# A fourth buffer for gathered U vectors, a later place for the last block's decoding, and no forced U work between the last G groups

## The chip, the cores and the metric

The kernel runs on one core of one Trainium2 chip. The metric is the device time of one execution in microseconds (us); three executions of the kernel before are at hand, and their median stands for it. Beside them there is one profiled execution, with a page and a trace: busy times, waits and the timeline of each engine. The engines are TensorE (PE, matmuls; PEld, its weight loads), VectorE (DVE), ScalarE (ACT), GpSimd (POOL, here an issuer of gathers) and SyncE (SP, which issues most transfers). Each works through its own list of instructions in the order in which the program emits them, and waits on semaphores for the others.

## The reference: what is computed

The program is one transformer-like layer on 512 tokens of width 1024 in float32: a layer norm, a mixer of 16 state-space heads and 8 latent-attention heads, a second norm, and a channel mixer with a residual and a last norm. The change touches the channel mixer, PEER, alone. It has 16384 experts; every token picks 16 of them in each of 8 heads.

```
q = (xb @ w_query)...; s = scores against 2 x 128 sub-keys
sv, si = lax.top_k(s, K)                          # 16 of 128, for both halves
top_s, top_pos = lax.top_k(cand_s, K)             # 16 of 256 candidate pairs
expert_idx = jnp.take_along_axis(cand_i, top_pos, axis=-1)
gate = jax.nn.softmax(top_s, axis=-1)
u = jnp.take(u_table, expert_idx, axis=0)
act = gelu(jnp.einsum('td,thkd->thk', xb, u))
v = jnp.take(v_table, expert_idx, axis=0)
return jnp.einsum('thk,thkd->td', gate * act, v)
```

So for token t the output is the sum over its 128 chosen experts e of gate * gelu(u_e . x_t) * v_e.

## The kernel before, in words

**Two ways to the same sum.** For the first three blocks of 128 tokens (384 tokens, NT) the kernel computes all experts densely: act = gelu(U x) for 128 chunks of 128 experts, times a matrix G of gates (zero where an expert wasn't chosen), times V. A float32 product is made of three matmuls of a high and a low part (mm3, L72 to L75). For the last block, and for the last 32 tokens (UG) of block 2 in the U step, the kernel gathers the rows of the tables that are needed and multiplies them on DVE. So a U matmul has 352 columns (NU), and V matmuls have 512 columns for three blocks and two halves.

**U chunk** (u_half, u_chunk, L1292 to L1305): 24 matmuls into one of two PSUM banks (pu), then a Gelu on ACT (L1301) that writes the act tile and frees the bank. **V chunk** (v_chunk, L1536): 18 matmuls into six banks that hold the sum over all 128 chunks. It needs P = act * G (DVE, L1493, and a small copy on ACT, L1495), the high part Ph (ACT, L1513) and the low part Pl (DVE, L1521). Weights for both come through one stream (Stream, L81): SP loads a tile of 128 x 1024 into one of three raw buffers (L92), ACT makes the high part (L110), DVE the low one (L120), two items ahead of PE.

**G, in 48 groups** (build_g, L1186): for each 8 tokens DVE makes one-hot matrices (L1194) and multiplies them with the gates (L1201); PE makes 16 small matmuls (L1220, L1221) into two PSUM tiles; ACT evicts them into a staging tile stg (L1223). For even groups from 2 to 42 (LOWA) DVE makes half of the product only, and ACT the other half with eight copies (L1226), issued behind the eviction of the group before. Every fourth group the staging tile is stored from ACT's queue, a small part to gs0 (L1229, 128 KB) and the rest to gsp (L1230, 1920 KB). V's stage reads them back, gt, four chunks at a time (load_g, L1401 to L1405; the first two loads read gs0).

**Gathered U vectors** (ug_index, ug_fetch, ug_dots, L1114 to L1144): 32 indirect transfers by POOL (L1130) into the tile urow with three buffers, and for each a product with a sum on DVE (L1136). The fetch that uses a buffer again is issued behind the product that frees it. One product is drawn per group, two in the groups 4, 8, 12, 16 and 20, and two earlier in the decoding. When all are done, their pool is closed and its room becomes a second pool for act tiles.

**Who orders the work.** The order of instructions is fixed when the program is built. drive (L1346) keeps two accounts in microseconds, tm[0] for PE and tm[1] for DVE: a U half chunk adds T_U/2 to the first, and its split 1.2 to the second; a group adds 0.95 to the first and 1.9 or 2.42 to the second, a gathered product 1.2. A half chunk is emitted as long as PE's account isn't ahead of DVE's, or, in build_g, as long as none has been emitted since the last group (least = 1). U chunks may go up to KEEP while one pool of act tiles exists and up to LEAD - RES = 54 with two.

**From G to V.** Behind the last group come, in the order of the program (L1465 to L1546): the loads for the decoding of block 3 (late3, L1101, decode, L1032: from L1105 and L1107), the first two gt loads, the decoding itself, dealt out by pump between U chunks 54 and 55, then P, Ph and Pl for V chunks 0 and 1, then pairs of a U chunk (from 56) and a V chunk (from 0). pump (L1241) draws so many microseconds (by the program's own figures) of the generator gather behind each chunk. When the decoding is done, gather goes on to 256 fetched rows for block 3 (L1431, five buffers), one DVE product each (L1442 for U, L1448 for V), spread over what remains of the U and V chunks (L1566 to L1571). The decoding uses Exp (L1060), the U chunks Gelu, and ACT loads a table between the two.

Of the kernel before, what the change touches and what calls it, by code (L numbers as in the profile page):

```python
# [11 lines left out]
F32 = mybir.dt.float32  # L12
# [19 lines left out]
UG = 32  # L32
NU = NT - UG
LEAD = 56
KEEP = 45
RES = 2
LASTC = 120
T_U = 3.87
T_Q = 6.3
ROWS = 5  # L40
ENDU = 12
# [13 lines left out]
def tile_block(ctx: ExitStack, tc: tile.TileContext, I, out):  # L55
# [1070 lines left out]

    def ug_fetch(n):
        if n < UG:
            UR[n] = ug.tile([128, D], F32, name="urow", bufs=3)
            G.indirect_dma_start(out=UR[n], out_offset=None, in_=I["u"],  # L1130
                                 in_offset=bass.IndirectOffsetOnAxis(ap=UR["ix"][:, n:n + 1], axis=0))

    def ug_dots():
        for n in range(UG):
            r = UR.pop(n)
            V.scalar_tensor_tensor(r, r, 1.0, UR["x"], op0=OP.mult, op1=OP.mult, accum_out=UR["hd"][:, n:n + 1])  # L1136
# [49 lines left out]
    def build_g():  # L1186
        jij = gb.tile([128, 4, 4, 128, 2], F16, name="ij")

        def hot(n):
            ijT, gT, gL = GT[n // 16]  # L1190
            r = n % 2
            col = ijT[:, n % 16 // 2, r].rearrange("p e (q c) -> p (e q) c", c=2)
            b2 = [128, 8, 128, 2]
            V.tensor_tensor(jij[:, 2 * r:2 * r + 2].rearrange("p e q i c -> p (e q) i c"), iotaE[:, None].to_broadcast(b2),  # L1194
                            col[:, :, None, :].to_broadcast(b2), op=OP.is_equal)
            oj, oi = jij[:, 1 + r], jij[:, 3 * r]
            g = gb.tile([128, 2, 4, 128, 2], F16, name="g", bufs=2)
# [3 lines left out]
            V.tensor_tensor(g[:, :ne], oi[:, None].to_broadcast(b4), gv[:, :, :, None, :].to_broadcast(b4), op=OP.mult)  # L1201
            low = [(g[:, 1, t // 2, :, t % 2], oi[:, t // 2, :, t % 2], gL[:, n % 16, t:t + 1]) for t in range(8)]
            return oj, g[:, 0], g[:, 1], low if ne == 1 else []

        nxt = hot(0)
        dots, head = UR["dots"], ug_head()
        tm[1] += 3.0
        yield 2.6
        for n in range(48):
            b, g = divmod(n, 16)  # L1210
            oj, oi, g1, _ = nxt
            if n < 47:
                nxt = hot(n + 1)
            if g % 4 == 0:
                stg = gs[n // 4 % 2].tile([128, 128, 32], F32, name="stg")
            for hf in range(2):
                ps = pw()
                for t in range(4):
                    q, c = hf * 2 + t // 2, t % 2
                    T.matmul(ps[:, t * 128:(t + 1) * 128], oj[:, q, :, c], oi[:, q, :, c], start=True, stop=False)  # L1220
                    T.matmul(ps[:, t * 128:(t + 1) * 128], oj[:, q, :, c], g1[:, q, :, c], start=False, stop=True)  # L1221
                q0 = g % 4 * 8 + hf * 4
                A.activation(stg[:, :, q0:q0 + 4],  # L1223
                             ps.rearrange("p (t i) -> p i t", t=4), AF.Copy, scale=1.0 / GSC)
            for o, i, z in nxt[3] if n < 47 else ():
                A.activation(o, i, AF.Copy, scale=z)  # L1226
# [105 lines left out]
    load_sk(0)  # L1332
    load_sk(1)
    tm = [0.0, 0.0]

    def step_u():
        e = len(UO)
# [55 lines left out]
    gb = pool("gb", side="right")  # L1393
    UR["w"] = gb.tile([UG, 128], F32, name="uw")
    UR["m"] = gb.tile([UG, 2], F32, name="um")
    drive(build_g(), 1)
    close(gb, *gs)
    vst = pool("vst")
    gt = {}
# [4 lines left out]
            src, q0 = (gs0, q * 4) if q < 2 else (gsp, q * 4 - 8)  # L1404
            nc.sync.dma_start(gt[q], src[:, :, q0:q0 + 4, :].rearrange("b j i t -> j b i t"))  # L1405

    GS = [-1, 0, 0]

    def gather():
        yield from late3()  # L1410
        ijg = IJG.pop(3)
        ix = gp_.tile([128, 128], I32, name="ix")
        f = lambda z: z.rearrange("p h k -> p (h k)")
        V.scalar_tensor_tensor(ix, f(ijg[:, 0]), 128.0, f(ijg[:, 1]), op0=OP.mult, op1=OP.add)
        g3 = gp_.tile([128, 128], F32, name="g3")
        V.tensor_copy(g3, f(ijg[:, 2]))
        close(*late, ijp)
        yield 0.5
        gp2 = pool("gp2", side="right")
        x3 = gp2.tile([128, D], F32, name="x3")  # L1420
        nc.sync.dma_start(x3, xsp[3])
        hd = gp2.tile([128, 128], F32, name="hd")
        ac = gp2.tile([128, D], F32, name="ac")
        V.memset(ac, 0.0)
        R = {}
        yield 0.1

        def fetch(s):
            if s < 256:
                R[s] = gp2.tile([128, D], F32, name="row", bufs=ROWS)  # L1430
                G.indirect_dma_start(out=R[s], out_offset=None, in_=I["u"] if s < 128 else I["v"],  # L1431
                                     in_offset=bass.IndirectOffsetOnAxis(ap=ix[:, s % 128:s % 128 + 1], axis=0))
# [103 lines left out]
    def v_chunk(c):  # L1536
# [4 lines left out]
        for b in range(3):  # L1541
            v_mm(b, c, hl)

    vc = 0
    for c in range(2):
        v_hi(c, v_prep(c))  # L1546
# [4 lines left out]
    while vc <= LASTC:  # L1551
# [171 lines left out]
```

## Time and profile before

| | |
|---|---|
| three executions | 1608.65, 1609.93, 1613.17 us |
| median | 1609.93 us |
| the profiled execution's own time | 1608.0 us |
| its span, first to last instruction | 1605.9 us |
| mean granted TensorE clock | 0.995 |
| U vectors gathered (first fetch to last product) | 561.4 to 707 us |
| groups of G on PE | 583.5 to 774 us |
| first V matmul | 798.8 us |
| PE busy in 700 to 750, 750 to 800, 800 to 850 us | 49.71, 35.05, 50.00 us |

How to read it: times in the trace count from the first instruction, so a point in the trace and the span compare directly, and the execution's own time is 2.1 us more. A row of the timeline has the start, the duration, the engine (SPq, ACTq and POOLq are the issuing sides of these engines), the line, the operation, and output and inputs by name. Brackets say how long the engine stood idle ahead of it and which instruction or transfer ended that. A row of a view by windows has, for each stretch, the busy time (and count) of PE, PEld, DVE, ACT and POOL, then the granted clock, the busy share of the transfer engines and GB/s. A row of waits has the waiting line, the line waited for, the total, the number and the longest. Matmul rows overlap: what counts for PE's pace is the distance of two starts.

### The profile page before, as it was taken

How to read it: one execution, taken by the hardware profiler on the slowest of the kernel's cores; microseconds unless marked ns; L12 is line 12 of the kernel's file. 1: busy time of each engine (PE TensorE's matmuls, PEld its weight loads, DVE VectorE, ACT ScalarE, POOL GpSimd, SP SyncE). 2: the span in 40 equal slices, each digit the busy share in tenths (PEclk: the TensorE clock that was granted, in tenths of full speed). 3: DMA queues.
4: the chain of work that ended last, by engine and by line, in shares of the span. 5: the costliest groups of instructions: out<-in, count | busy, mean ns of one | idle time of the engine just before them, and what ended most of it. 6: DMA issues, size and time to landing. Idle time of an engine off the chain costs nothing.

```text
span 1605.9 us, 24098 instructions
## 1 busy us (share of the span) xinstructions
PE 1572.7 (98%) x8699; PEld 1381.7 (86%) x8699; DVE 1344.6 (84%) x2545; ACT 754.8 (47%) x1409; POOL 547.7 (34%) x400
## 2 busy tenths in 40 slices
PE   9999999999999999999699999999999999999997
PEld 7887888887888999989599999999999999888886
DVE  8978677647799998989678888888888888988887
ACT  5564467731333457779433343333333433433342
POOL 0000032500245134410045555555555455544310
PEclk9999999999999999999899999999999999999999
DMA  6342132473433479887599999999999999999974
GB/s 248 97 155 91 47 78 64 138 249 118 134 93 91 142 244 343 330 307 255 202 333 344 362 346 349 340 354 355 338 338 365 343 337 356 372 327 351 327 254 143
DMA packets 154556, 403.88 MB, mean 251 GB/s; under 512 B 13037, under 2 KB 65965, under 8 KB 152645
## 3 DMA queue, kind: packets, MB, share of 16 engines
q1 hardware_dynamic: 104948, 213.19, 39.7%
q0 software_dynamic: 45888, 163.73, 27.9%
q10 hardware_dynamic: 3600, 25.43, 4.0%
q8 instruction: 68, 1.11, 0.3%
q14 instruction: 52, 0.42, 0.1%
HBM read 368.40 MB, written 31.80 MB: 249 GB/s over the span
## 4 chain that ended last, share of the span: by engine, by line
PE 77%; DVE 11%; issue 5%; ACT 2%; POOL 2%; DMA 2%; DVEq 0%; SPq 0%; ACTq 0%; POOLq 0%
PE va L1530 11%; PE va L1531 11%; PE va L1534 11%; PE pu L73 8%; PE pu L75 8%; PE pu L74 8%; PE pa L74 3%; PE pa L75 3%; PE pa L73 3%; POOL urow L1130 2%; PE pw L74 1%; PE pw L75 1%; PE pw L73 1%; DVE t L1003 1%; DVE ti L1007 1%
## 5 line engine op out<-in xcount | busy, mean ns | idle before, releaser
L110 ACT ACTIVATE wih<-wir 128x1024 fp32r<-128x1024 f32 (+2 forms) x269 | 277.7, 1033 | 279.2 <-DMA wir<-v 113.5
L120 DVE TENSOR_TENSOR wil<-wir,wih 128x1024 fp32r<-128x1024 f32 (+1 forms) x235 | 284.1, 1210 | 97.9 <-ACT wih L110 40.0
L75 PE MATMUL pu<-XTH,wil 128*128 128x352 f32 x1008 | 325.2, 323 | 0.5 <-DVE wil L120 0.5
L73 PE MATMUL pu<-XTH,wih 128*128 128x352 f32 x896 | 292.8, 327 | 5.8 <-ACT act L1301 5.8
L74 PE MATMUL pu<-XTL,wih 128*128 128x352 f32 x896 | 289.3, 323 | 0.0
L1531 PE MATMUL va<-wil,Ph 128*128 128x512 f32 x726 | 283.6, 391 | 0.0
L1431 POOL DMA_INDIRECT row<-u,ix x128 | 191.6, 1497 | 215.5 <-DVE row L1442 138.6
L1431 POOL DMA_INDIRECT row<-v,ix x128 | 183.5, 1434 | 191.6 <-DVE ac L1448 170.2
L75 PEld LDWEIGHTS pu<-XTH,wil 128*128 128x128 f32 x1008 | 190.0, 188 | 0.9 <-DVE wil L120 0.9
L73 PEld LDWEIGHTS pu<-XTH,wih 128*128 128x128 f32 x896 | 168.8, 188 | 10.1 <-ACT act L1301 6.4
L1530 PE MATMUL va<-wih,Ph 128*128 128x512 f32 x438 | 171.5, 392 | 4.5 <-ACT Ph L1513 4.5
L74 PEld LDWEIGHTS pu<-XTL,wih 128*128 128x128 f32 x896 | 169.0, 189 | 2.8
L1448 DVE SCALAR_TENSOR_TENSOR ac<-row,hd,ac 128x1024 f32<-128x1024 f32 x128 | 164.0, 1281 | 2.7 <-DMA row<-v,ix 0.6
L1531 PEld LDWEIGHTS va<-wil,Ph 128*128 128x128 f32 x726 | 136.7, 188 | 26.0
L1442 DVE SCALAR_TENSOR_TENSOR row<-row,x 128x1024 f32<-128x1024 f32 x128 | 150.1, 1221 | 2.8 <-DMA row<-u,ix 2.8
L1301 ACT ACTIVATE act<-pu 128x352 f32<-128x352 f32 x126 | 58.2, 462 | 167.3 <-PE pu L75 162.9
L1534 PE MATMUL va<-wih,Pl 128*128 128x512 f32 x438 | 135.3, 390 | 0.0
L110 ACT ACTIVATE wihx<-wir 128x1024 fp32r<-128x1024 f32 x67 | 71.0, 1059 | 121.0 <-DMA wir<-v 84.8
L120 POOL TENSOR_TENSOR wil<-wir,wih 128x1024 fp32r<-128x1024 f32 (+3 forms) x34 | 70.5, 2081 | 154.5 <-PE pw L75 100.2
L1530 PE MATMUL va<-wihx,Ph 128*128 128x512 f32 x288 | 112.3, 390 | 0.0
L120 DVE TENSOR_TENSOR wil<-wir,wihx 128x1024 fp32r<-128x1024 f32 x62 | 75.8, 1223 | 41.0 <-issue 27.9
L1530 PEld LDWEIGHTS va<-wih,Ph 128*128 128x128 f32 x438 | 82.5, 188 | 20.7 <-ACT Ph L1513 4.8
(500 smaller groups left out, 3230.6 us busy)
## 6 DMA issues: line engine op xcount, KB each, us to landing
wir<-ut SPq DMA_DIRECT2D x128, 512.0 KB
wir<-v SPq DMA_DIRECT2D x128, 512.0 KB
gsp<-stg ACTq DMA_DIRECT2D x12, 1920.0 KB
gt<-gsp SPq DMA_DIRECT2D x30, 768.0 KB
wir<-wo SPq DMA_DIRECT2D x26, 512.0 KB
wir<-wf SPq DMA_DIRECT2D x18, 512.0 KB
wir<-wqr SPq DMA_DIRECT2D x16, 512.0 KB
de<-acd POOLq DMA_DIRECT2D x8, 512.0 KB
```

Of the source, the lines that this page charges most:

```text
L73: T.matmul(ps, lh, rh, start=start, stop=False)
L74: T.matmul(ps, lh, rl, start=False, stop=False)
L75: T.matmul(ps, ll, rh, start=False, stop=stop)
L110: A.activation(h, r, AF.Copy)
L120: self.lo(n).tensor_tensor(l, r, h, op=OP.subtract)
L1301: A.activation(ACT[c], ps, AF.Gelu)
L1431: G.indirect_dma_start(out=R[s], out_offset=None, in_=I["u"] if s < 128 else I["v"], in_offset=bass.IndirectOffsetOnAxis(ap=ix[:, s % 128: ...
L1442: V.scalar_tensor_tensor(r, r, 1.0, x3, op0=OP.mult, op1=OP.mult, accum_out=hd[:, s:s + 1])
L1448: V.scalar_tensor_tensor(ac, r, hd[:, s - 128:s - 127], ac, op0=OP.mult, op1=OP.add)
L1530: T.matmul(va[b][e], Ph[b], h[:, cs], start=c == 0, stop=False)
L1531: T.matmul(va[b][e], Ph[b], l[:, cs], start=False, stop=False)
L1534: T.matmul(va[b][e], Pl[b], h[:, cs], start=False, stop=c == 127)
```

## The change

One more buffer for gathered U vectors (UROWS = 4), so the first act pool has 42 tiles in place of 45 and the second 14 in place of 11; the two-product groups become 2, 5, 8, 11, 14 and 17; T_U is 3.9 in place of 3.87. From group 32 on no half chunk is forced between groups (least becomes 0). The generator of block 3's decoding and gathering starts behind V's chunk 0 and not ahead of U chunk 54: the gt loads come first on SP, U chunks 54 and 55 follow with nothing between them, and the first pump is the one in V's loop, at 2.1 us for a chunk and 4.2 for a pair. The definitions of load_g to v_chunk move up unchanged, and are left out below.

```diff
-KEEP = 45
+KEEP = 42
+UROWS = 4
-T_U = 3.87
+T_U = 3.9
...
-        for n in range(3):
+        for n in range(UROWS):
             ug_fetch(n)
...
-            UR[n] = ug.tile([128, D], F32, name="urow", bufs=3)
+            UR[n] = ug.tile([128, D], F32, name="urow", bufs=UROWS)
...
-            ug_fetch(n + 3)
+            ug_fetch(n + UROWS)
...
             tm[0] += 0.95
+            if n == 32:
+                least[0] = 0
...
-            for _ in range(2 if n in (4, 8, 12, 16, 20) else 1):
+            for _ in range(2 if n % 3 == 2 and n < 18 else 1):
                 tm[1] += next(dots, 0.0)
...
-    def drive(fill, least=0):
+    def drive(fill):
...
-            if (tm[0] <= tm[1] or n < least) and un[0] < (LEAD - RES if len(aps) > 1 else KEEP):
+            if (tm[0] <= tm[1] or n < least[0]) and un[0] < (LEAD - RES if len(aps) > 1 else KEEP):
...
-    drive(build_g(), 1)
+    least[0] = 1
+    drive(build_g())
...
+    for q in range(2):
+        load_g(q)
+    if UO:
+        step_u()
+    uc = un[0]
+    while uc < LEAD:
+        u_chunk(uc)
+        uc += 1
+    close(psW)
+    close(psX)
...
     gp_ = pool("gp")
     fill = gather()
-    next(fill)
-    for q in range(2):
-        load_g(q)
-    if UO:
-        step_u()
-    pump(fill, 2.5)
-    uc = un[0]
-    while uc < LEAD:
-        u_chunk(uc)
-        uc += 1
-        pump(fill, 4.0)
-    close(psW)
-    close(psX)
...
         if GS[0] < 0:
-            more = pump(fill, 1.9 * w)
+            more = pump(fill, 2.1 * w)
```

More of the change, by code (lines that the diff above doesn't have):

```diff
@@ L1334, in tile_block @@
     tm = [0.0, 0.0]
+    least = [0]
     def step_u():
@@ L1405, in load_g, with v_prep @@
             nc.sync.dma_start(gt[q], src[:, :, q0:q0 + 4, :].rearrange("b j i t -> j b i t"))
+    for q in range(2):
[8 more added lines that the diff above has]
+    close(psX)
+    psV = pool("psV", space=PSUM)
+    va = [[psV.tile([128, 512], F32, name=f"va{b}{e}") for e in range(2)] for b in range(3)]
+    PP = {}
+    pend, last = [], {}
+    def v_prep(c):
+        load_g(c // 4)
+        if c % 4 == 0:
+            load_g(c // 4 + 1)
+        a = ACT.pop(c)
+        P = vst.tile([128, NT], F32, name="P", bufs=2)
+        V.tensor_tensor(P[:, :NU].rearrange("p (b t) -> p b t", t=32), a.rearrange("p (b t) -> p b t", t=32),
+                        gt[c // 4][:, :NU // 32, c % 4, :], op=OP.mult)
+        A.activation(P[:, NU:], gt[c // 4][:, NU // 32, c % 4, :], AF.Copy)
+        if c % 4 == 3:
+            gt.pop(c // 4)
+        return P
@@ new lines, in v_sb, with v_hi @@
+    def v_sb(c, nm):
+        if c > LASTC:
+            t = act_tile().bitcast(F32R)
+            if nm == "Ph":
+                x = act_tile().bitcast(F32R)
+                last[c] = x[:, 128:256]
+                return ((t[:, :256], 0, 256), (x[:, :128], 256, NT))
+            return ((t[:, :256], 0, 256), (last.pop(c), 256, NT))
+        return ((vst.tile([128, NT], F32R, name=nm, bufs=3), 0, NT),)
+    def v_hi(c, P):
+        Ph = v_sb(c, "Ph")
+        for t, a, b in Ph:
+            A.activation(t, P[:, a:b], AF.Copy)
+        pend.append((c, P, Ph))
@@ new lines, in v_lo, with v_mm @@
+    def v_lo():
+        if pend:
+            c, P, Ph = pend.pop()
+            Pl = v_sb(c, "Pl")
+            for (t, a, b), (h, _, _) in zip(Pl, Ph):
+                V.tensor_tensor(t, P[:, a:b], h, op=OP.subtract)
+            blk = lambda z: [t[:, i:i + 128] for t, a, b in z for i in range(0, b - a, 128)]
+            PP[c] = (blk(Ph), blk(Pl))
+    def v_mm(b, c, hl, es=(0, 1)):
+        Ph, Pl = PP[c]
+        h, l = hl
+        for e in es:
+            cs = slice(e * 512, (e + 1) * 512)
+            T.matmul(va[b][e], Ph[b], h[:, cs], start=c == 0, stop=False)
+            T.matmul(va[b][e], Ph[b], l[:, cs], start=False, stop=False)
+        for e in es:
+            cs = slice(e * 512, (e + 1) * 512)
+            T.matmul(va[b][e], Pl[b], h[:, cs], start=False, stop=c == 127)
@@ L1407, in tile_block, with v_chunk @@
+    def v_chunk(c):
+        v_lo()
+        P = v_prep(c + 2)
+        hl = item()
+        v_hi(c + 2, P)
+        for b in range(3):
+            v_mm(b, c, hl)
     GS = [-1, 0, 0]
@@ L1466, in tile_block @@
     fill = gather()
-    next(fill)
-    for q in range(2):
-        load_g(q)
-    if UO:
-        step_u()
-    pump(fill, 2.5)
-    uc = un[0]
-    while uc < LEAD:
-        u_chunk(uc)
-        uc += 1
-        pump(fill, 4.0)
-    close(psW)
-    close(psX)
-    psV = pool("psV", space=PSUM)
-    va = [[psV.tile([128, 512], F32, name=f"va{b}{e}") for e in range(2)] for b in range(3)]
-    PP = {}
-    pend, last = [], {}
-    def v_prep(c):
-        load_g(c // 4)
-        if c % 4 == 0:
-            load_g(c // 4 + 1)
-        a = ACT.pop(c)
-        P = vst.tile([128, NT], F32, name="P", bufs=2)
-        V.tensor_tensor(P[:, :NU].rearrange("p (b t) -> p b t", t=32), a.rearrange("p (b t) -> p b t", t=32),
-                        gt[c // 4][:, :NU // 32, c % 4, :], op=OP.mult)
-        A.activation(P[:, NU:], gt[c // 4][:, NU // 32, c % 4, :], AF.Copy)
-        if c % 4 == 3:
-            gt.pop(c // 4)
-        return P
@@ L1500, in v_sb @@
-    def v_sb(c, nm):
-        if c > LASTC:
-            t = act_tile().bitcast(F32R)
-            if nm == "Ph":
-                x = act_tile().bitcast(F32R)
-                last[c] = x[:, 128:256]
-                return ((t[:, :256], 0, 256), (x[:, :128], 256, NT))
-            return ((t[:, :256], 0, 256), (last.pop(c), 256, NT))
-        return ((vst.tile([128, NT], F32R, name=nm, bufs=3), 0, NT),)
-    def v_hi(c, P):
-        Ph = v_sb(c, "Ph")
-        for t, a, b in Ph:
-            A.activation(t, P[:, a:b], AF.Copy)
-        pend.append((c, P, Ph))
@@ L1516, in v_lo @@
-    def v_lo():
-        if pend:
-            c, P, Ph = pend.pop()
-            Pl = v_sb(c, "Pl")
-            for (t, a, b), (h, _, _) in zip(Pl, Ph):
-                V.tensor_tensor(t, P[:, a:b], h, op=OP.subtract)
-            blk = lambda z: [t[:, i:i + 128] for t, a, b in z for i in range(0, b - a, 128)]
-            PP[c] = (blk(Ph), blk(Pl))
-    def v_mm(b, c, hl, es=(0, 1)):
-        Ph, Pl = PP[c]
-        h, l = hl
-        for e in es:
-            cs = slice(e * 512, (e + 1) * 512)
-            T.matmul(va[b][e], Ph[b], h[:, cs], start=c == 0, stop=False)
-            T.matmul(va[b][e], Ph[b], l[:, cs], start=False, stop=False)
-        for e in es:
-            cs = slice(e * 512, (e + 1) * 512)
-            T.matmul(va[b][e], Pl[b], h[:, cs], start=False, stop=c == 127)
@@ L1536, in v_chunk @@
-    def v_chunk(c):
-        v_lo()
-        P = v_prep(c + 2)
-        hl = item()
-        v_hi(c + 2, P)
-        for b in range(3):
-            v_mm(b, c, hl)
     vc = 0
```

## The prediction

> **What bounds the kernel now.** I read the page's busy times first, then the stretches by window, then the waits of PE, and last the timeline around the one hole that these show.
>
> ```profile
> span 1605.9 us, 24098 instructions
> PE 1572.7 (98%) x8699; PEld 1381.7 (86%) x8699; DVE 1344.6 (84%) x2545; ACT 754.8 (47%) x1409; POOL 547.7 (34%) x400
> ```
> ```profile
> 750.00:800.00 50.00, 35.05 (x282) 32.20 (x282) 35.65 (x50) 26.49 (x56) 1.16 (x2) 0.92 0.60 214
> 800.00:850.00 50.00, 50.00 (x258) 45.06 (x258) 39.07 (x56) 20.98 (x36) 25.61 (x17) 0.97 0.94 329
> 798.00:1530.00 732.00, 731.23 (x3716) 651.37 (x3717) 623.09 (x794) 283.80 (x485) 375.16 (x257) 1.00 0.96 345
> ```
> ```profile
> PE pu L73 <- ACT act L1301: 5.8, 2, 5.6
> PE pw L1220 <- DVE g L1201: 5.6, 4, 1.7
> PE va L1530 <- ACT Ph L1513: 4.5, 1, 4.5
> ```
>
> PE sets the time: it is idle for 1605.9 - 1572.7 = 33 us in all, and the V stage (798 to 1530) leaves it 0.8 us. Nearly half of the idle time, 50 - 35.05 = 15 us, lies in one window, 750 to 800, where the granted clock also falls to 0.92 (the column behind POOL's). The three longest waits are all there, but for 1.3 us of the second. So what the change can win is in that hole, and what it can lose is any place where PE, now full, gets a new one.
>
> ```profile
> 781.38 0.32 PE L75 MATMUL pu<-XTH,wil 128*128 128x352 f32 x1
> 787.33 0.66 PE L73 MATMUL pu<-XTH,wih 128*128 128x352 f32 x1 [5.63 <-ACT act L1301]
> ...
> 793.90 0.32 PE L75 MATMUL pu<-XTH,wil 128*128 128x352 f32 x1
> 798.77 0.50 PE L1530 MATMUL va<-wih,Ph 128*128 128x512 f32 x1 [4.55 <-ACT Ph L1513]
> ...
> 804.61 0.33 PE L73 MATMUL pu<-XTH,wih 128*128 128x352 f32 x1
> ...
> 808.45 0.40 PE L1530 MATMUL va<-wihx,Ph 128*128 128x512 f32 x1
> ...
> 812.57 0.33 PE L73 MATMUL pu<-XTH,wih 128*128 128x352 f32 x1
> ```
>
> Here U chunk 55 ends at 781.38 + 0.16 = 781.54 (matmuls start 0.16 apart). Chunk 56 starts at 787.33, V chunk 0 at 798.77, U chunk 57 at 804.61. At full clock a U chunk takes 808.45 - 804.61 = 3.84 and a V chunk 812.57 - 808.45 = 4.12. So 781.54 to 804.61, 23.07 us, holds 3.84 + 4.12 = 7.96 us of work: **the hole costs 15.1 us**, about 10 of it idle, the rest slow matmuls behind each gap.
>
> ```profile
> 781.15 1.28 ACT L1060 ACT_TABLE_LOAD   x1 [6.53 <-DMA gsp<-stg]
> ...
> 786.81 0.46 ACT L1301 ACTIVATE act<-pu 128x352 f32<-128x352 f32 x1
> ...
> 789.12 0.23 ACT L1495 ACTIVATE P<-gt 128x32 f32<-128x32 f32 x1
> ```
> ```profile
> 781.87 0.41 SPq L1107 DMA_DIRECT2D ts<-ts  x1
> ...
> 783.60 1.28 SPq L1405 DMA_DIRECT2D gt<-gs  x2
> ```
> ```profile
> 783.92 0.29 DVE L1037 TENSOR_TENSOR dd<-ts 128x128 f32<-128x128 f32 x1 [11.11 <-DMA ts<-ts]
> ...
> 797.58 0.52 DVE L1493 TENSOR_TENSOR P<-act,gt 128x352 f32<-128x352 f32 x1
> 798.75 0.56 DVE L1521 TENSOR_TENSOR Pl<-P,Ph 128x384 fp32r<-128x384 f32 x1 [0.65 <-ACT Ph L1513]
> ```
>
> The reader sees the reason on the other engines. The decoding of block 3 (late3, L1107 to L1086) waits for the last store of G to leave its staging tile. Its Exp stands on ACT ahead of the Gelu (L1301) that frees chunk 56's PSUM bank; its vector work, 783.92 to 797.58, stands on DVE ahead of the first P (L1493). Both gaps are queue order, not work that PE needs.
>
> **The change, part by part.** *Decoding behind V's first products.* U chunks 54 to 56 then need nothing of late3 and run on to 781.54 + 3.84 = 785.4. V chunk 0 needs P, so gt 0. Its load is the first thing on SP, and reads what the last small store (L1229) wrote. That store is out at the latest with the large one, at 781.1 by ACT's wait; gt 0, issued at 783.60, was there by 789.12, at most 5.5 us. So gt 0 lands by 786.6 at the latest, and P, Ph (0.65 + 0.52) put V chunk 0 at 787.8: 0 to 2.4 us late. I take 0.5, since the small store is issued ahead of the large one and the 5.5 is itself an upper bound.
>
> The moved step still has to be paid: 783.92 to 797.58 less two splits of 1.2 is 11.2 us of DVE, two table loads on ACT, five loads on SP and the fetches on POOL behind them. It is dealt out at 2.1 x 2 = 4.2 us of the program's own account for each pair of a U and a V chunk, so over four pairs, 4 x 7.96 = 31.8 us of PE. DVE's own work in a pair is two splits, a Pl and a P.
>
> ```profile
> L120 DVE TENSOR_TENSOR wil<-wir,wih 128x1024 fp32r<-128x1024 f32 (+1 forms) x235 | 284.1, 1210 | 97.9 <-ACT wih L110 40.0
> ```
>
> That is 2 x 1.21 + 0.56 + 0.52 = 3.5, over four pairs 14.0; with 11.2 it makes 25.2 of 31.8. PE hides it, with one new wait: the first decoding instruction (L1037) waits on DVE for ts. Queued behind it are the splits of U 58 and V 2 and their P, and PE for these; behind the Exp on ACT stand the next wih, Ph and Gelu. The wait was 783.92 - 781.87 = 2.05 us on an empty queue; behind weight loads I bound it by gt's 5.5. PE has a pair in hand (7.96 us, against 3.5 of DVE work and the wait), so a short wait costs nothing and a long one up to 5 us with the table loads. I take 0.5, near the empty-queue row.
>
> *The buffers.* KEEP falls from 45 to 42: U work may go no further than chunk 42 before the gathered vectors' pool closes. Carrying the program's two accounts forward (PE: 0.95 a group, T_U/2 a half chunk; DVE: 1.9 or 2.42 a group, 1.2 a dot and a split) gives the order of issue. Before, chunk 45 is reached just as the pool closes, in group 25, and the limit of 54 behind group 43, so that 44 to 47 run bare. The trace has that order, three bare groups waiting at its end:
>
> ```profile
> 692.55 1.22 DVE L1136 SCALAR_TENSOR_TENSOR urow<-urow,ux 128x1024 f32<-128x1024 f32 x1 [2.54 <-DMA urow<-u,uix]
> ```
> ```profile
> 697.37 0.23 PE L1220 MATMUL pw<-g,ij 128*128 128x128 f16 x1 [1.34 <-DVE g L1201]
> ```
> ```profile
> 768.08 0.23 PE L1220 MATMUL pw<-g,ij 128*128 128x128 f16 x1 [1.66 <-DVE g L1201]
> ```
> ```profile
> 770.47 0.23 PE L1220 MATMUL pw<-g,ij 128*128 128x128 f16 x1 [1.30 <-DVE g L1201]
> ...
> 772.87 0.23 PE L1220 MATMUL pw<-g,ij 128*128 128x128 f16 x1 [1.31 <-DVE g L1201]
> ```
> ```profile
>   DMA urow<-u,uix: 8.6, 5
> ```
>
> After, chunk 42 is reached behind group 21 and the pool closes in group 24: nothing stands between groups 22, 23 and 24. The same sum puts no U work ahead of 33, 34, 36 and 41 either. Behind group 32, say, PE's account stands at 317.85 and DVE's at 316.82, so no half chunk is added where before one was forced; behind 33 it is 318.80 against 318.72. And it still reaches 54 behind group 43: the last four stay bare, so there the change doesn't do what its words say, except that both halves of chunk 53 now stand ahead of group 44.
>
> DVE's 8.6 us of waits for gathered vectors should go, but PE felt only 1.34 of them: **-1.3**.
>
> *Bare groups.* An even group up to 42 takes half of its right side from eight copies on ACT, which stand behind the eviction of the group before.
>
> ```profile
> 728.03 0.22 PE L1221 MATMUL pw<-g,ij 128*128 128x128 f16 x1
> ...
> 730.07 0.23 PE L1220 MATMUL pw<-g,ij 128*128 128x128 f16 x1
> ...
> 731.33 0.22 PE L1221 MATMUL pw<-g,ij 128*128 128x128 f16 x1
> ```
> ```profile
> 729.38 1.89 ACT L1226 ACTIVATE g<-ij,gL 128x128 f16<-128x128 f16 x6
> ```
>
> From the last matmul of group 31 to that of group 32 pass 3.30 us with the copies running to 731.27, though half a U chunk (2.01) lay between: 0.4 was lost. Bare, the same 3.30 holds 0.9 of PE work: 2.4 lost. Groups 34 and 36 thus cost 2.0 more each, **+4.0**. Group 24 had a whole chunk ahead of it and lost nothing; bare it loses 2.4 at least. At most DVE has no lead and does two groups (2.4 each, by the spacing 768.08, 770.47) and two dots of 1.22 while PE has 1.8: 5.4. DVE did have a lead of 2.54 - 1.34 = 1.2 there, and more once its earlier waits are gone: I take **+2.8**. In the tail, with a whole chunk ahead of group 44, group 45 is ready; two waits of 2.4 - 0.9 = 1.5 replace 1.66 + 1.30 + 1.31: **-1.3**.
>
> *The clock.* It fell after 5.63 and 4.55 us of idling and not after 1.66. My new gaps are at most 2.4 in one piece, so I charge nothing. [...]
>
> **Sum.** -15.1 + 0.5 + 0.5 - 1.3 + 4.0 + 2.8 - 1.3 = -9.9 us. The profiled execution took 1608.0 (span 1605.9 and 2.1 around it) and would take 1598.1; the median of the runs shown, 1609.93, lies 1.9 above it, so the forecast is **1600.0**.
>
> **The rivals.** *The bare groups cost nothing,* since DVE and ACT gain a lead over a PE that has more U work at once: the 4.0 and the 2.8 fall away, 1600.0 - 6.8 = 1593.2. For it speaks that DVE is freed of 8.6 us of waits in the same stage; against it, that the copies follow the eviction, which no lead moves, so that a part of it (to 1597) is likelier than the whole.
>
> *The decoding stalls V's first chunks.* With 5 us there instead of 0.5, and gt 0 late by 2.4: 1600.0 + 4.5 + 1.9 = 1606.4. For it speaks that DMA runs at 0.94 in 800 to 850; against it that DVE there is busy 39 of 50.
>
> *V is bound by its transfers, and the time rises.* The fetches start four pairs later, behind the decoding.
>
> ```profile
> L1431 POOL DMA_INDIRECT row<-u,ix x128: 933/1677/1992, 798.5 to 1152.5; - x128
> L1431 POOL DMA_INDIRECT row<-v,ix x128: 933/1299/2585, 1154.5 to 1527.5; - x128
> ```
> ```profile
> GB/s 248 97 155 91 47 78 64 138 249 118 134 93 91 142 244 343 330 307 255 202 333 344 362 346 349 340 354 355 338 338 365 343 337 356 372 327 351 327 254 143
> ```
>
> The first fetch would move from 798.5 to about 785.4 + 3.8 x 7.96 = 816. If the 729 us of fetching couldn't be pressed, they would end 17 us later and the kernel with them: 1627. It decides if more than 345 GB/s can't be sustained at a DMA share of 0.96; 256 rows of 128 x 1024 f32 (0.52 MB) over some 26 us less need 6 to 7 GB/s more. Against it: one slice moved 372 with PE full, so the rival gets little. [...]
>
> **How the numbers follow.** Forecast (1597 to 1604) 0.55; bare groups free, wholly or in part (1593 to 1597) 0.12; stalls in V (1604 to 1609) 0.19; transfers bind (about 1627) 0.09; else 0.05. The range 1593.0 to 1607.5 takes in the first two and 0.12 of the third, 0.79. A measurement of this kernel can tell about 0.3%, 4.8 us, from no change: below 1605.1 lie 0.55 + 0.12 + 0.06 = 0.73; between 0.13 and 0.02 of else, 0.15; above 0.09 + 0.03 = 0.12.
>
> **What would show it.** Right: PE's waits for act (5.6) and Ph (4.5) are gone or below 1, no clock below 1 near the start of V, urow waits near 0, PE gaps of 2 to 3 us ahead of or within groups 24, 34, 36 and two of about 1.5 ahead of the last two. Wrong: waits of V's first matmuls for wil or Ph behind L1037, DVE waiting for rows by tens of us in V, or a fall of the clock in the bare groups.

## The result and the profile after

The changed kernel takes 1602.94 us, the median of 12 executions (1600.44 to 1606.56); 12 of the kernel before have a median of 1610.82 (1608.65 to 1613.17). The ratio is 0.9954, with a 95% interval of 0.9945 to 0.9963: faster by 7.9 us, where 9.9 were forecast. The profiled execution took 1602.0, 6.0 less than the profiled one of before.

First the page's busy times, then the stretches by window (PE, PEld, DVE, ACT and POOL busy, granted clock, share and rate of the transfers), then PE's waits:

```profile
span 1600.2 us, 24088 instructions
PE 1576.7 (99%) x8699; PEld 1386.3 (87%) x8699; DVE 1343.8 (84%) x2545; ACT 754.5 (47%) x1409; POOL 554.6 (35%) x400
```
```profile
700.00:750.00 50.00, 47.45 (x382) 42.83 (x382) 36.97 (x40) 36.40 (x90) 1.05 (x2) 0.97 0.61 215
750.00:800.00 50.00, 46.98 (x373) 44.43 (x373) 32.78 (x33) 31.70 (x69) 0.00 (x0) 0.93 0.70 232
800.00:850.00 50.00, 50.00 (x269) 45.71 (x268) 41.20 (x66) 23.50 (x37) 16.19 (x11) 1.00 0.78 267
798.00:1530.00 732.00, 732.00 (x3728) 652.14 (x3727) 635.02 (x818) 288.23 (x491) 381.98 (x258) 1.00 0.96 349
```
```profile
PE pw L1221 <- DVE g L1202: 4.1, 3, 1.7
PE pw L1221 <- ACT g L1227: 1.9, 1, 1.9
...
PE pw L1222 <- ACT g L1227: 1.0, 1, 1.0
...
PE pu L74 <- ACT act L1304: 0.4, 1, 0.4
```

(The lines of the code have moved: PE's matmuls of the groups are L1221 and L1222 now, U's L74 to L76, V's L1472 to L1476, the gt loads L1410, P L1435.) A group is called bare here when no U work stands ahead of it. PE is busy for 46.98 us in the window that had 35.05: the waits of 5.6 for act and 4.5 for Ph are gone. New are two waits for ACT's copies (L1227), and 700 to 750, which had 49.71 of PE, has 47.45. PE is busy for 4 us *longer* in the whole span than before, with the same 8699 matmuls, and the clock stands at 0.97 and 0.93 in the two windows: some of them ran slowly. The V stage is full, as it was.

The timeline of PE has the bare group 24 and the U chunk behind it, and then the tail with V chunk 0:

```profile
693.69 0.22 PE L1222 MATMUL pw<-g,ij 128*128 128x128 f16 x1
695.76 0.23 PE L1221 MATMUL pw<-g,ij 128*128 128x128 f16 x1 [1.85 <-ACT g L1227]
...
697.55 0.27 PE L1222 MATMUL pw<-g,ij 128*128 128x128 f16 x1
697.57 0.64 PE L74 MATMUL pu<-XTH,wih 128*128 128x352 f32 x1
698.01 0.49 PE L75 MATMUL pu<-XTL,wih 128*128 128x352 f32 x1
698.30 0.49 PE L76 MATMUL pu<-XTH,wil 128*128 128x352 f32 x1
...
699.98 0.32 PE L76 MATMUL pu<-XTH,wil 128*128 128x352 f32 x1
```
```profile
776.97 0.23 PE L1221 MATMUL pw<-g,ij 128*128 128x128 f16 x1 [1.66 <-DVE g L1202]
...
779.36 0.29 PE L1221 MATMUL pw<-g,ij 128*128 128x128 f16 x1 [1.30 <-DVE g L1202]
...
781.01 0.64 PE L74 MATMUL pu<-XTH,wih 128*128 128x352 f32 x1
...
794.53 0.40 PE L1472 MATMUL va<-wih,Ph 128*128 128x512 f32 x1
...
798.65 0.33 PE L74 MATMUL pu<-XTH,wih 128*128 128x352 f32 x1
```

Group 24 ends 3.86 us behind group 23 (697.55 - 693.69), with 0.9 of work: 3.0 lost. Behind it U's matmuls start 0.29 apart, not 0.16, until about 699.9: PE is at half its clock although it is waiting for nothing. U chunk 57 starts at 798.65 and not at 804.61. Those 6.0 us are the whole gain: the spans differ by 5.7, so next to nothing is won or lost behind it.

Stretches cut by the clock (the third figure from the end of a row) show where it fell, in the kernel after and then in the same stretches of before:

```profile
697.00:701.00 4.00, 4.00 (x21) 3.83 (x20) 3.34 (x3) 2.51 (x6) 0.79 (x1) 0.64 0.96 399
...
744.00:748.00 4.00, 3.98 (x17) 3.77 (x17) 3.86 (x9) 2.43 (x5) 0.00 (x0) 0.57 1.16 430
...
778.00:785.00 7.00, 5.70 (x32) 5.64 (x31) 2.41 (x3) 2.98 (x5) 0.00 (x0) 0.53 0.41 161
785.00:800.00 15.00, 15.00 (x87) 14.26 (x87) 6.10 (x8) 5.76 (x12) 0.00 (x0) 0.99 0.96 286
```
```profile
697.00:701.00 4.00, 3.63 (x33) 3.63 (x34) 3.97 (x6) 1.26 (x3) 0.00 (x0) 1.00 0.72 237
...
744.00:748.00 4.00, 4.00 (x36) 3.87 (x36) 3.90 (x7) 3.58 (x8) 0.50 (x1) 1.00 1.04 434
...
778.00:785.00 7.00, 3.70 (x24) 3.40 (x22) 0.94 (x6) 2.04 (x3) 0.00 (x0) 1.00 0.52 192
785.00:800.00 15.00, 7.66 (x28) 6.70 (x29) 13.68 (x24) 5.13 (x11) 1.16 (x2) 0.75 0.59 174
```

Each fall begins in bare groups (24, 36, and 45 to 47) and lasts into what stands behind them. The clock records in the trace give the same three: half clock for 3.41 us from 696.46, for 3.41 from 744.25 and for 6.83 from 778.38. Before, the clock fell only at the two long waits of the hole (5.63 and 4.55), for 6.83 us from 785.64 and for 3.41 from 799.29. (Both traces have one more fall at the very end: in the last 10 us of the span the granted clock is 0.70 in the change and 0.78 before.)

### The profile page after: what moved, and what is told of

It reads as the page before. It is cut to its first block, busy times and chain, and to the rows that moved or that the text cites. A ratio compares the mean times of both kernels' runs of the same rounds, so it can differ in the third digit from the quotient of the medians.

```text
span 1600.2 us, 24088 instructions
## 1 busy us (share of the span) xinstructions
PE 1576.7 (99%) x8699; PEld 1386.3 (87%) x8699; DVE 1343.8 (84%) x2545; ACT 754.5 (47%) x1409; POOL 554.6 (35%) x400
## 4 chain that ended last, share of the span: by engine, by line
PE 83%; DVE 12%; ACT 3%; DMA 1%; issue 1%; DVEq 0%; ACTq 0%
PE va L1473 10%; PE va L1472 10%; PE va L1476 10%; PE pu L74 10%; PE pu L75 10%; PE pu L76 10%; PE pa L75 3%; PE pa L76 3%; PE pa L74 3%; PE pw L75 1%; PE pw L1222 1%; PE pw L76 1%; PE pw L74 1%; DVE t L1004 1%; PE pw L1221 1%
## 5 line engine op out<-in xcount | busy, mean ns | idle before, releaser
L121 DVE TENSOR_TENSOR wil<-wir,wih 128x1024 fp32r<-128x1024 f32 (+1 forms) x235 | 284.2, 1210 | 102.6 <-ACT wih L111 46.0
L76 PE MATMUL pu<-XTH,wil 128*128 128x352 f32 x1008 | 325.8, 323 | 0.0
L74 PE MATMUL pu<-XTH,wih 128*128 128x352 f32 x896 | 293.9, 328 | 0.4 <-ACT act L1304 0.4
L1510 POOL DMA_INDIRECT row<-v,ix x128 | 188.8, 1475 | 174.8 <-DVE ac L1527 149.2
L76 PEld LDWEIGHTS pu<-XTH,wil 128*128 128x128 f32 x1008 | 190.7, 189 | 0.0
L74 PEld LDWEIGHTS pu<-XTH,wih 128*128 128x128 f32 x896 | 169.7, 189 | 4.7 <-ACT act L1304 0.7
L1472 PE MATMUL va<-wih,Ph 128*128 128x512 f32 x438 | 170.7, 390 | 0.0
L1476 PE MATMUL va<-wih,Pl 128*128 128x512 f32 x438 | 134.9, 389 | 0.0
L121 POOL TENSOR_TENSOR wil<-wir,wih 128x1024 fp32r<-128x1024 f32 (+3 forms) x34 | 70.5, 2081 | 154.7 <-PE pw L76 100.2
L1472 PE MATMUL va<-wihx,Ph 128*128 128x512 f32 x288 | 112.3, 390 | 0.0
L121 DVE TENSOR_TENSOR wil<-wir,wihx 128x1024 fp32r<-128x1024 f32 x62 | 75.8, 1222 | 32.0 <-issue 17.2
L1476 PEld LDWEIGHTS va<-wih,Pl 128*128 128x128 f32 x438 | 82.2, 188 | 17.3
```

The lines of the kernel that those rows point to most:

```text
L74: T.matmul(ps, lh, rh, start=start, stop=False)
L76: T.matmul(ps, ll, rh, start=False, stop=stop)
L121: self.lo(n).tensor_tensor(l, r, h, op=OP.subtract)
L1472: T.matmul(va[b][e], Ph[b], h[:, cs], start=c == 0, stop=False)
L1476: T.matmul(va[b][e], Pl[b], h[:, cs], start=False, stop=c == 127)
```

## The experiments

Theory: the change is two things of opposite sign. Moving the decoding wins about what the hole cost; taking away the forced U work makes bare groups, which cost PE waits and, beyond what was forecast, its clock. Rivals: the buffers (and the vectors' waits) are what won; the clock falls for some other reason; V is near a limit that the late decoding uses up.

| kernel | executions | median us | ratio to before, 95% interval |
|---|---|---|---|
| the change | 12 | 1602.94 | 0.9954, 0.9945 to 0.9963 |
| the move alone | 5 | 1598.21 | 0.9919, 0.9898 to 0.9939 |
| all but the move | 11 | 1615.11 | 1.003, 1.002 to 1.004 |
| the change, U work still forced | 5 | 1596.49 | 0.9913, 0.9893 to 0.9933 |
| the change, bare groups filled | 5 | 1600.24 | 0.9936, 0.9914 to 0.9957 |
| U work spread evenly | 4 | 1592.19 | 0.9889, 0.9874 to 0.9904 |
| spread, three chunks kept back | 5 | 1598.36 | 0.9928, 0.9914 to 0.9941 |
| forced, decoding dealt out at once | 10 | 1609.35 | 0.9993, 0.9984 to 1.0002 |
| forced, decoding dealt out slowly | 10 | 1604.20 | 0.9958, 0.9942 to 0.9974 |

**The move alone.** The changed kernel with everything else put back:

```diff
-KEEP = 42
-UROWS = 4
-T_U = 3.9
+KEEP = 45
+UROWS = 3
+T_U = 3.87
...
-            if n == 32:
-                least[0] = 0
...
-            for _ in range(2 if n % 3 == 2 and n < 18 else 1):
+            for _ in range(2 if n in (4, 8, 12, 16, 20) else 1):
```

> Only the move of block 3's decoding behind V's first products; buffers, limit, account and forcing stay as before. Theory: the move alone wins the whole hole (15.1 us) less about 1.3 us that V's first P waits for gt, and the other edits give a part of it back; so about 1597, faster than the whole change (1602.9), with no half clock ahead of V. Rival: the move brings only what the whole change brought (about 8 us, the rest being lost in V), and the other edits are neutral or gain; then 1602 to 1604.

Measured: 1598.21, 12.1 less than before (1610.34 in the same runs). The move alone is faster than the whole change. One part of the theory failed: there is half clock ahead of V (0.93 in 750 to 800, as in the change), behind the bare groups 44 to 47, which this kernel has in common with the one before.

**All but the move.** The kernel before with all of the change that was put back above, the uses of UROWS and of least with it:

```diff
-KEEP = 45
-T_U = 3.87
+KEEP = 42
+UROWS = 4
+T_U = 3.9
...
             tm[0] += 0.95
+            if n == 32:
+                least[0] = 0
...
-            for _ in range(2 if n in (4, 8, 12, 16, 20) else 1):
+            for _ in range(2 if n % 3 == 2 and n < 18 else 1):
```

> Everything but the move: four buffers, limit 42, spread products, unforced last groups, with the decoding ahead of V as before. Theory: bare groups 24, 34 and 36 cost about 7 us in place of the 1.3 us wait for a gathered vector, the tail wins 1.3, and half-clock windows behind the bare groups add 2 to 3: 4 to 7 us slower than before, about 1616. Rival: these edits are neutral or a gain: 1608 to 1611.

Measured: 1615.11, 4.8 more than before. Its waits of PE:

```profile
PE pu L74 <- ACT act L1304: 7.0, 2, 6.0
PE pw L1221 <- DVE g L1202: 5.2, 4, 1.7
PE va L1535 <- ACT Ph L1518: 5.0, 1, 5.0
...
PE pw L1222 <- ACT g L1227: 1.0, 1, 1.0
```

The hole's two waits are back at their size (6.0 and 5.0). The groups' waits come to 6.2, where before had 5.6; the larger part of the loss is in PE's busy time, 1577.9 us for 1572.7 before, in slow and thinly spaced matmuls (granted clock 0.97 in 700 to 750, where before had 1.00). The two halves add up: -12.1 + 4.8 = -7.3, against -7.9 for the whole. So the rest of the change gives back more than a third of what the move wins.

**U work still forced.** Of the rest, only the last of its edits is undone:

```diff
-            if n == 32:
-                least[0] = 0
```

> The whole change, but one half chunk of U stays forced between all groups. Theory: groups 34 and 36 have their half chunk again; the 4 us that they cost and the half-clock window behind 36 (1.4) go: about 1597.5, 5 us below the whole change. Rival: the bare groups only shift work that PE has to do anyway, so nothing changes: 1602 to 1604.

Measured: 1596.49, 6.4 less than the change and the same as the move alone within the intervals. So the unforced groups are what costs; the fourth buffer and the other spreading of the products can't be told from nothing here.

**Bare groups filled.** Twenty matmuls of 128 columns, into a PSUM tile that nobody reads, are added behind groups 23, 33, 35, 45 and 46. They do no useful work.

```diff
+            if n in (23, 33, 35, 45, 46):
+                if n == 23:
+                    fl = px()
+                for _ in range(20):
+                    T.matmul(fl[:, 0:128], oj[:, 0, :, 0], oi[:, 0, :, 0], start=True, stop=True)
             for o, i, z in nxt[3] if n < 47 else ():
```

> The whole change, with 20 small matmuls of no use (1.15 us, into a spare PSUM tile that nobody reads) behind each of the groups 23, 33, 35, 45 and 46, where PE stands idle. Theory: the gaps themselves stay as long, but PE works in them, so the clock isn't halved behind them; that takes away about 5 us of slow matmuls and gives back some 1.3 that V's first product then waits for gt: about 1599. Rival: the clock follows something else than PE's idling, and the halvings stay: 1602 to 1605.

Measured: 1600.24, 2.7 less than the change, with a hundred matmuls *more*. The intervals overlap, so the time alone doesn't prove the gain; the granted clock does tell the two apart. The last window before V, and PE's wait there:

```profile
750.00:800.00 50.00, 48.11 (x407) 45.08 (x405) 30.21 (x31) 30.67 (x65) 0.00 (x0) 1.00 0.76 247
```
```profile
PE va L1477 <- ACT Ph L1460: 1.2, 1, 1.2
```

The clock is 1.00 where it was 0.93, and it is 1.00 in each window from 650 to 850. That isn't one lucky trace: the mean granted clock of the five executions is 0.997 to 0.999, of the change's twelve 0.993 to 0.997, and three of the five are faster than all twelve. So PE's sparse work in the bare groups is what lowers it. Whether a single gap or the thin work around it counts, this run can't tell, since filling also shortens the gaps (ahead of group 24 from 1.85 to 0.73). It also uncovers a wait that the slow clock had hidden: V chunk 0 now waits 1.2 for Ph.

**U work spread evenly.** From group 22 on exactly one half chunk behind each group, but none behind 24, 30, 34 and 38 (all followed by odd groups, for which ACT has no copies to make), and the two-product groups are the odd ones below 18.

```diff
-T_U = 3.9
+T_U = 3.87
...
-            for _ in range(2 if n % 3 == 2 and n < 18 else 1):
+            for _ in range(2 if n % 2 and n < 18 else 1):
...
-            if n == 32:
-                least[0] = 0
+            if n >= 22:
+                most[0] = least[0] = 0 if n in (24, 30, 34, 38) else 1
...
-    least = [0]
+    least, most = [0], [99]
...
-            if (tm[0] <= tm[1] or n < least[0]) and un[0] < (LEAD - RES if len(aps) > 1 else KEEP):
+            if (tm[0] <= tm[1] and n < most[0] or n < least[0]) and un[0] < (LEAD - RES if len(aps) > 1 else KEEP):
```

> The whole change, but the U half chunks are spread by hand over what follows the closing of the gathered vectors' pool: two gathered products in every odd group up to 17, so that the pool closes in group 21; from group 22 on exactly one half chunk behind each group, none behind 24, 30, 34 and 38, so that only odd groups (which need no copies from ACT) stand bare and the last four have U work ahead of them. Theory: the losses at group 24 (2.8, and 1.4 of half clock) and the tail's two waits (3.0) go, while V's first product still waits about 1.2 us for gt: 5 to 7 us below the forced variant (1596.5), 1590 to 1592. Rival: DVE's own work in these groups (about 60 us for 22 groups against 58.5 of PE) is the bound, so the waits only move: 1595 to 1597.

Measured: 1592.19, the best of all kernels in the table: 10.7 less than the change and 18.7 less than before. First the busy times, then the two waits that it has left around here:

```profile
span 1589.9 us, 24090 instructions
PE 1568.7 (99%) x8699; PEld 1378.8 (87%) x8699; DVE 1342.2 (84%) x2545; ACT 755.0 (47%) x1409; POOL 550.1 (35%) x400
```
```profile
PE pw L1221 <- DVE g L1202: 2.6, 4, 1.3
...
PE va L1472 <- ACT Ph L1455: 1.1, 1, 1.1
```

PE's busy time for the same 8699 matmuls fell from 1576.7 to 1568.7. So 8.0 of the 10.3 between the two spans is matmuls that take less long, most of it clock (the change's three falls are 13.65 us at half clock, and this kernel has none ahead of its end: 1.00 in each window from 650 to 850), and only 2.3 is waiting. The bare groups that are left here are odd ones and stand one at a time.

**Three chunks kept back.** The evenly spread kernel, with one more U chunk left to stand ahead of V:

```diff
-RES = 2
+RES = 3
...
-                most[0] = least[0] = 0 if n in (24, 30, 34, 38) else 1
+                most[0] = least[0] = 0 if n in (24, 28, 32, 34, 38, 42) else 1
```

> The spread variant with three U chunks in place of two kept back for the time behind the last group (two more odd groups bare). Theory: V's first product has 3.8 us more cover and no longer waits for gt (1.2 us won), but the groups have 3.8 us less PE work to cover DVE's, which costs 1 to 3 there: within 2 us of the spread variant. Rival: gt's wait is not what V's start hangs on, then the start moves by nothing.

Measured: 1598.36, 6.2 worse, where no more than 2 was expected. The groups wait 4.8 for DVE in place of 2.6, which is within the 1 to 3 that were expected. Most of the rest is at V's start. On ACT there:

```profile
786.55 1.06 ACT L111 ACTIVATE wih<-wir 128x1024 fp32r<-128x1024 f32 x1 [8.29 <-DMA wir<-ut]
```

The extra chunk's weights are loaded behind the two gt loads on SP. ACT stands 8.29 us for them, ahead of the Ph that V chunk 0 needs, and PE waits 3.25 for that Ph, where it waited 1.1, and runs at half clock for 3.41 us behind it (0.97 in 750 to 800). Cover for one wait had made another: the order of the loads on SP mattered more than the length of the cover. Ahead of that wait the clock is whole (1.00 in 700 to 750), although PE is busy for only 46.54 us there, less than the change's 47.45 at 0.97.

**Decoding dealt out at once, and slowly.** Both with U work still forced. The step in V's loop becomes 8.4 (the decoding is over in about one pair), or 0.8 (it goes on for some ten pairs, and the row fetches start late).

```diff
-            more = pump(fill, 2.1 * w)
+            more = pump(fill, 8.4 * w)
```

> The forced variant, with the moved decoding dealt out four times as fast (8.4 us of the program's account for a chunk, 16.8 for a pair), so that all of it stands behind the first pair. Theory: DVE then does 11 us of decoding and its wait for ts at one go while PE has about 8 us in hand: PE waits 4 to 8 us for a split of U 58 or for V 2, with half clock behind it: 1601 to 1606. Rival: V's weights and P are prepared far enough ahead, so nothing is lost: 1595 to 1598.

Measured: 1609.35, 12.9 more than at 2.1: what the move won is gone. PE's longest wait:

```profile
PE pu L76 <- DVE wil L121: 10.8, 1, 10.8
```

A weight split (L121) stood behind the whole decoding on DVE. The mechanism is the one foreseen, half clock behind the wait included (13.65 us by the records, most of it within the wait; 0.86 in 800 to 850). The price is near double the middle of the range of 4.5 to 9.5, since the wait was 10.8 and not 4 to 8.

```diff
-            more = pump(fill, 2.1 * w)
+            more = pump(fill, 0.8 * w)
```

> The forced variant, with the moved decoding dealt out at 0.8 us for a chunk (1.6 for a pair), so that it ends, and the fetching of rows starts, some six pairs (about 50 us) later and the rows come some 7% denser. Theory: transfers and DVE have room, V stays full: 1595 to 1599. Rival: V is bound by its transfers, then denser rows make DVE wait for them and PE for DVE: above 1605.

Measured: 1604.20, but with executions from 1595.98 to 1610.24, evenly between: neither forecast. The V stage of the change, then of the profiled one of these (which took 1598.91), and ACT there at one of its waits:

```profile
850.00:1450.00 600.00, 600.00 (x3097) 538.31 (x3096) 521.17 (x668) 231.82 (x392) 331.91 (x222) 1.00 0.98 356
```
```profile
850.00:1450.00 600.00, 597.38 (x3071) 535.10 (x3070) 526.38 (x682) 229.43 (x390) 341.05 (x232) 1.00 0.98 361
```
```profile
1359.41 1.06 ACT L111 ACTIVATE wih<-wir 128x1024 fp32r<-128x1024 f32 x1 [7.71 <-DMA wir<-v]
```

With the same rows to fetch in less time, the transfers move 361 GB/s in place of 356. A weight tile comes late in the middle of V (the row at 1359.41), PE waits 2.6 there, and its clock falls for 3.41 us (the starts behind the wait stand 0.43 apart, and 0.23 later). So at 361 GB/s there is a wait that the change, at 356 with PE full in the same 600 us, doesn't have. This trace is of one of the fastest of the ten; that the slower ones lost more in the same way is likely, but not shown.

**The last large store, earlier.** In the evenly spread kernel the last store to gsp is sent behind group 43 and not behind 47, so it leaves out the gates of the last groups, and only its timing counts.

```diff
-                nc.scalar.dma_start(gsp[b * 4 + g // 4], stg[:, 8:])
+                if n < 47:
+                    nc.scalar.dma_start(gsp[b * 4 + g // 4], stg[:, 8:])
+                if n == 43:
+                    nc.scalar.dma_start(gsp[11], stg[:, 8:])
```

> The evenly spread kernel, with the last large store of G (1920 KB) sent behind group 43 instead of behind group 47. It then sends group 43's staging tile, since the last one isn't full yet, so the last eight tokens-by-chunk entries of block 2 hold gates of an earlier group: that part of G is changed. Theory: the first two gt loads take 9.0 us from issue to use, instead of at most 5.5 before, because they share the transfer engines with that store, issued 1.4 us ahead of them. With the store 8 us earlier the first P should come at most 6.5 us behind the issue of gt, V chunk 0 should find Ph there (its wait of 1.1 us is gone), and the span should be about 1 us shorter (1589 +- 1.5). Rival: the gt loads are slow by themselves (two loads in pieces of 512 B, issued over 3.4 us) or wait for the small store: then the 9.0 us and the wait of 1.1 us stay, whatever the large store does.

Measured (one execution, 1591.09): a span of 1589.3 against 1589.9. The gt loads and the first P, first with the store in its place, then with it early:

```profile
774.04 3.42 SPq L1410 DMA_DIRECT2D gt<-gs  x2
```
```profile
783.05 0.52 DVE L1435 TENSOR_TENSOR P<-act,gt 128x352 f32<-128x352 f32 x1 [6.29 <-DMA gt<-gs]
```
```profile
776.70 2.13 SPq L1413 DMA_DIRECT2D gt<-gs  x2
```
```profile
782.20 0.52 DVE L1438 TENSOR_TENSOR P<-act,gt 128x352 f32<-128x352 f32 x1 [5.97 <-DMA gt<-gs]
```
```profile
SPq L1413 <- DMA gs<-stg: 9.4, 1, 9.4
```

From issue to use pass 9.0 us beside the store and 5.5 without it, so the rival falls that the loads are slow by themselves: in these two executions they are slow where the large store is beside them. The gain isn't shown: the loads were issued 2.7 later, because SP now waited (last row) for the *small* store of group 47. That store was issued at 771.7, behind two large ones. V chunk 0 still waits 0.8 where it waited 1.1. The store's traffic is moved, not removed.

## Why the prediction was right, and where it was not

**The hole (-15.1): right.** PE has no wait for act or Ph left there. From U chunk 54 at 781.01 to U chunk 57 at 798.65 pass 17.64 us; three U chunks and a V chunk need 3 x 3.84 + 4.12 = 15.64, and the 2.0 above that is clock. The move alone measured -12.1 for a sum of -14.1 (-15.1 and the two terms of 0.5), its tail at half clock among it.

**V chunk 0 waits for gt (+0.5): 0 here, by luck.** The step said "at most 5.5 us" from issue to use, from a load that had no large store beside it. Here it is issued 1.4 behind that store:

```profile
783.72 3.40 SPq L1410 DMA_DIRECT2D gt<-gs  x2
```
```profile
792.78 0.53 DVE L1435 TENSOR_TENSOR P<-act,gt 128x352 f32<-128x352 f32 x1 [4.45 <-DMA gt<-gs]
```

That is 9.1 us. PE didn't wait only because U chunk 54 ran at half clock and V chunk 0 came due 2.0 later; where the clock is whole, the wait is 1.1 to 1.2 (filled, forced and evenly spread kernels).

**The decoding in V's first pairs (+0.5): right, at 0.** DVE stood 4.08 us for its first load, inside the bounds of 2.05 and 5.5, and no matmul waited:

```profile
803.91 0.29 DVE L1038 TENSOR_TENSOR dd<-ts 128x128 f32<-128x128 f32 x1 [4.08 <-DMA ti<-ti]
```

The two pump runs show that this is a matter of rate. Dealt out at 4.2 a pair it is free, in one piece it costs a wait of 10.8. The first row fetch came at 825.5, not 816, and V took it.

**The vectors (-1.3): right.** DVE's waits for gathered vectors, 8.6 before, are gone from the list of waits, and with them PE's 1.34. But as said at that place, PE had felt only that much.

**Bare groups (+4.0 and +2.8) and the tail (-1.3): right within 0.6.** Group 24 lost 3.0 for 2.8. Groups 34 and 36 cost 2.4 and 2.0 more than when covered, for 2.0 each, by the same sum over their rows. The tail's two waits are 1.66 + 1.30 = 2.96 for 3.0.

**The clock (0): wrong, and the largest error.** The step was "My new gaps are at most 2.4 in one piece, so I charge nothing". The gaps were as small as that, 1.0 to 1.9, and the clock still halved three times; a fall in the bare groups was one of the prediction's own signs of being wrong. By the spacing of the starts it cost 1.1 behind group 24 (697.57 to 699.98: 2.41 for eight steps of 0.16), 1.5 behind 36, and 2.7 in group 47 and behind it (2.0 of them the excess above): **about 5.3 us**. The terms as measured come to -15.1 - 1.3 + 4.4 + 3.0 - 1.3 + 5.3 = -5.0; the profiled execution shows -6.0, and the last 1.0 isn't placed. The filled kernel shows the cause: with the same chain of work on DVE and ACT, but PE kept busy in it, the clock stays whole. The length of the longest single gap doesn't decide: a fall came behind a gap of 0.98 (group 36), and none behind 1.66 and 1.30 in the tail of the kernel before. The two kernels whose bare groups are all odd ones and stand one at a time from group 21 on (evenly spread, and three chunks kept back) have no fall up to the end of the groups (1.00 in both windows from 650 to 750). How little work it takes for a fall isn't settled.

The same stretch doesn't bring a fall each time. The forced kernel and its two versions with another rate of decoding run the same instructions until V has begun, and in all three the tail waits 1.66 and 1.30. The window over the tail, first of the forced kernel, then with the decoding at once, then slowly:

```profile
750.00:800.00 50.00, 45.86 (x365) 42.41 (x364) 31.47 (x38) 31.17 (x68) 0.00 (x0) 1.00 0.72 248
```
```profile
750.00:800.00 50.00, 46.99 (x349) 44.03 (x348) 30.56 (x40) 29.51 (x63) 0.00 (x0) 0.93 0.71 239
```
```profile
750.00:800.00 50.00, 45.90 (x355) 42.62 (x354) 33.00 (x35) 29.49 (x62) 0.00 (x0) 1.00 0.76 259
```

The first has its fall behind group 24 (3.41 us from 698.74), the second in the tail (6.83 from 772.62), the third in neither place. In the same way the kernel before kept its clock over its bare groups at the end (waits of 1.66, 1.30 and 1.31), and the move alone, with the same groups bare, lost it (0.93 in 750 to 800). So the program alone doesn't settle whether a fall comes. In the change's records the three falls begin whole steps of 3.413 us apart (47.79 and 34.13 us, 14 and 10 of them); what decides between a fall and none, no run shows. The 5.3 is therefore the price in one execution. For all twelve there is only the mean clock: with medians of 0.9945 for the change and 0.998 filled, the difference is 0.0035 of 1602 us, 5.6 us, an estimate of the same size.

**The number.** That 1602.94 lies within the range is in part luck. Between the two profiled executions 6.0 were won, 3.9 less than forecast. The medians differ by 7.9, because the profiled execution of before lay 2.8 below its median of twelve and that of the change 0.9 below.

**The rivals.** Bare groups cost something, so the first fell. The decoding didn't stall V at the rate chosen, but does at four times it. Of the third rival's transfer limit the slowly dealt run has a sign, a PE wait at 361 GB/s, 1.4% above the change's 356; in the change itself nothing waited. The prediction's 345, and the 6 to 7 that it adds, are means over the whole stage, which the late start of the fetches thins out: over 798 to 1530 the change moved 349.

## What to carry to other kernels

A full engine that others feed can lose twice in a stretch where it has little to do: by its waits, and by its clock (here 3.0 and 1.1 us at group 24). So spread its independent work one piece to each such stretch, and don't take short gaps as proof that the clock holds: here it fell behind gaps of 0.98 to 1.85 us. A step off the bounding engine can be moved behind the point that it delays at no cost, as long as it is dealt out in pieces that fit the cover there: here no matmul waited for it at 4.2 us a pair, and in one piece it brought a wait of 10.8 and cost as much as the move had won. A duration read from a lone transfer can be too short beside a large store (here 5.5 us, and 9.0 beside it), so ask of each load that is brought forward what else is moving then.

## What was not expected of the hardware

- PE's clock halved behind stretches whose gaps were 1.0 to 1.9 us, and stayed down for 3.41 or 6.83 us by the records, with PE busy for most of that time (3.41 of 3.41, 3.39 of 3.41 and 5.85 of 6.83 us). A hundred useless matmuls in those stretches kept it whole, and the median was 2.7 us lower.
- The same instructions with the same waits (1.66 and 1.30) brought a fall in one execution and none in two others.
- Two gt loads of 768 KB took 9.0 us from issue to use beside a 1920 KB store and 5.5 without it; and a store of 128 KB, issued at 771.7 behind two large ones, held back the loads that wait for it until 776.7, 5.0 us, where the median of its kind from issue to landing is 1.8.
- V's transfers ran at 356 GB/s over 600 us with PE never waiting, and at 361 with one weight tile so late that PE waited 2.6. Single slices of 40 us moved more, up to 379 on the page of the changed kernel:

```profile
GB/s 249 97 154 93 47 78 59 140 246 126 123 97 88 142 240 371 352 255 196 270 242 365 373 350 358 334 379 358 336 354 365 357 344 358 371 353 334 343 256 141
```
